# Two-layer hybrid decoder trunk: token norm in the operands of the mixer's second and later projections, convolution taps read from PSUM, o tiles before the convolved ones

## The chip, the cores and the metric

The kernel runs on one core of one Trainium2 chip. The metric is the device time of one execution in microseconds (us). The core's engines are TensorE (PE; its weight loads appear as PEld), VectorE (DVE), ScalarE (ACT), GpSimd (POOL) and SyncE (SP, which here only issues loads and stores).

## What is computed

Input `x` has 512 tokens of width 1024. Each of two layers does

```
x += 1/2 * SwiGLU(RMSNorm(x))
x += W_out [ sparse-attention heads | mLSTM heads ](RMSNorm(x) @ W_in)
x += 1/2 * SwiGLU(RMSNorm(x))
```

The mixer (the second line) is what the change touches. In the reference, cut to what matters:

```
q, k, v, q_idx, k_idx, w_idx, qk_m, v_m, o_m, i_pre, f_pre = split_columns(h @ w_in)      # h = rmsnorm(x, g)
att = dsa_attention(rope(rmsnorm(q)), rope(rmsnorm(k)), v, rope(q_idx), rope(k_idx), w_idx)  # top-128 keys per query
qk_m = silu(causal_conv(qk_m, conv_w, conv_b))                                            # 4 taps along the tokens
h_m = mlstm(q_m, k_m, v_m, i_pre + b_i, f_pre + b_f)                                      # 4 heads, chunks of 128
h_m = rmsnorm(h_m, m_norm) * sigmoid(o_m)
return concatenate([att, h_m]) @ w_out
```

with `rmsnorm(x, g) = x * rsqrt(mean(x*x) + eps) * g`. The factor `rsqrt(...)` is one number per token, the gain `g` one per channel.

## The kernel before

**Layout.** `x` is held transposed, eight tiles `x[i]` of 128 channels x 512 tokens. Every fp32 matmul is done as three matmuls (`mm3`, line 296) over operands split in a high and a low part (`hi`, `lo`; `whi`, `wlo` for weights, `yh`, `yl` for the normed input). Weights come in units of 128 x 1024. SP loads each unit into `raw`; ACT rounds it to `whi`; `wlo` is made by DVE, or (units marked for it, all of the mixer but the first four) by an ACT copy and a load that POOL issues and that adds the weights to it (`unit`, line 263).

**The mixer** (`mixer`, line 545) runs in this order:

1. `norm` (line 315): per tile ACT squares `x[i]` and writes `yh = x*g`, DVE writes `yl = x*g - yh`, POOL adds the squares up in `acc`. The gain is in these operands, the token factor isn't.
2. `proj_a` (index and key columns, gates), `proj_q`, `proj_v`: each a `proj_tok` (line 574), four weight units of 8 tile pairs. In these the tokens are the output partitions. The token factor `rs` (one per partition) is applied when ACT takes the result out of PSUM.
3. Twelve `proj_chan` (line 921), one weight unit and 24 matmuls each, in the order `HEADS` (line 36): four o tiles and, per head, one tile for q and one for k. Here the tokens are the free dimension, and DVE multiplies the result by `rsb`, the token factor spread over all partitions. For an o tile ACT then takes a tanh (`proj_o`, line 931). For q and k (`proj_qk`, line 941) the product lands in a padded SBUF tile `cv`, ACT applies the last tap and the bias, DVE adds three taps, and ACT and DVE make the silu.
4. `out_proj` (line 1064) of the attention half, then of the mLSTM half, each 16 groups of 6 matmuls per half; DVE adds into `x`.

**What sets the order.** PE's instructions keep the order in which the program issues them; the other engines' are ordered by a scheduler that goes by program order, priorities and estimated times. Beside the main line there are threads (generators): the tail of the norm, `front` (index and key tiles, scores), `gates`, `qprep`, `select` (top 128 by 8 at a time), `attention`, and one `mlstm` per head. The main line calls `tick()` after every 6 matmuls, and each thread then runs on to its next `yield n`, which lets it sleep for n ticks (`LAG`, line 34). So the threads' PE instructions stand between those of the projections, at places counted in ticks. `drain()` and `join()` run ticks without matmuls of the main line.

The threads that matter here:

- `scale` (line 342) starts 12 ticks after `norm` (`LAG["norm"]`): four matmuls (eight PE instructions) over `acc`, `rsqrt` on DVE (11 small steps), four diagonal tiles; 3 ticks later a matmul spreads them, and ACT writes `rsb`.
- `front`: `prep(b)` rotates and splits the index and key columns of one block of 128 tokens into `stk` tiles; `flip` transposes them on PE. `prep(0)` is issued at tick 17, its flips at tick 24.
- `attention`: logits on PE, mask and minimum on DVE, exponential on ACT, transposes on PE, a copy `pT` on ACT, and two ticks after the transposes the product with v into `op`. Block results go to `zah`, `zal`.
- `mlstm(l, h)` (line 967) is spawned when both convolved tiles of head h are issued and waits until the head before it has got through. Its PE steps are `mb` at once, the two products on the convolved tiles 4 ticks later (`cv`), the chunk states 2 later, the first pair of outputs `hn` 2 later, the second pair 1 later. Then DVE and ACT normalize `hn` to `hm`, and 10 ticks after the second pair PE transposes `hm` (line 1054); from that `zh`, `zl`, the operands of the second half of the output projection, are made. The transposes also wait until all o and convolved tiles are issued.

PSUM: four banks `mm` serve the projections and `mlstm`, three `aux`, one `op`.

Of the kernel before, what the change touches and what calls it, by code (L numbers as in the profile page):

```python
# [7 lines left out]
F32 = mybir.dt.float32  # L8
F32R = mybir.dt.float32r
I32 = mybir.dt.int32  # L10
AF = mybir.ActivationFunctionType
ALU = mybir.AluOpType
# [3 lines left out]
P = 128  # L16
S = 512
# [3 lines left out]
NKT = D // P  # L21
# [5 lines left out]
MH, MD = 4, 128  # L27
# [3 lines left out]
FILL = -3.3e38  # L31
MARK = -3.4e38
UN = 1024
LAG = {"norm": 12, "prep": 3, "prep2": 4, "f0": 1, "q0": 12, "qprep": 5, "att": 2, "ml": 2, "cv": 4, "hm": 9,
       "gates": 16, "ffn": 6, "ffn0": 10, "bc": 4, "g": 5, "fl": 1, "sc": 1, "attend": 3, "np": 1}
HEADS = (("o", 0), ("qk", 0), ("qk", 1), ("qk", 2), ("o", 1), ("qk", 3), ("o", 2), ("o", 3))
PLAIN = ((0, 0), (0, 1), (1, 0), (1, 1))
H = S // 2
WARM = 16
# [5 lines left out]
POOLC = (0, 0)  # L45
# [14 lines left out]
class Trunk:  # L60
# [484 lines left out]
    def mixer(self, l):  # L545
        self.norm(self.gm[l])
        self.flips = 0
        self.fronted = False
        self.chosen = {0}
        self.conv = {}  # L550
        self.hm = {}
        self.z = {}
        self.va = None
        self.zatt = None
        self.attended = 0
        self.proj_a(l)
        self.proj_q(l)
        self.proj_v()
        self.ml = 0
        self.join(lambda: self.fronted)  # L560
        self.so = {}
        for nm, h in HEADS:
            if nm == "o":
                self.proj_o(h)
            else:
                self.proj_qk(l, h, 0)
                self.proj_qk(l, h, 1)
                self.spawn(self.mlstm(l, h))
        self.join(lambda: self.attended == NB)
        self.out_proj([(self.zatt[0][:, i, :], self.zatt[1][:, i, :]) for i in range(4)])  # L570
        self.drain()
        self.out_proj([self.z[h] for h in range(MH)])

    def proj_tok(self, n):
        ps = [self.pm.tile([P, S], F32, name="mm", tag="mm") for _ in range(NB)]
# [201 lines left out]
    def proj_q(self, l):  # L777
        nc = self.nc
        ps = self.proj_tok(512)
        self.qT = self.ap_.tile([P, AH, S], F32R, name="qT", tag="qT")  # L780
        qa = []
        for b in range(NB):
            qa.append(self.ap_.tile([P, S], F32, name="qa", tag="s4a", bufs=4))
            nc.scalar.activation(qa[b], ps[b], AF.Copy, scale=self.rs[:, b:b + 1])
        self.spawn(self.qprep(qa))

    def qprep(self, qa):
# [124 lines left out]
    def proj_v(self):  # L912
        nc = self.nc
        ps = self.proj_tok(512)
        self.va = self.ap_.tile([P, NB, MH, MD + 1], F32, name="va", tag="big")
        nc.gpsimd.memset(self.va[:, :, :, MD:MD + 1], 1.0)
        for b in range(NB):
            nc.scalar.activation(self.va[:, b, :, 0:MD], ps[b].rearrange("p (h d) -> p h d", d=MD), AF.Copy,
                                 scale=self.rs[:, b:b + 1])

    def proj_chan(self):
        hi, lo = self.unit()
# [8 lines left out]
    def proj_o(self, h):  # L931
        nc = self.nc
        ps = self.proj_chan()
        if h % 2 == 0:
            self.so2 = self.ap_.tile([P, 2, S], F32, name="so", tag="so", bufs=2)
        so = self.so2[:, h % 2, :]
        nc.vector.tensor_tensor(out=so, in0=ps, in1=self.rsb, op=ALU.mult)
        nc.scalar.activation(so, so, AF.Tanh, scale=0.5)
        self.so[h] = so

    def proj_qk(self, l, h, i):
        nc = self.nc
        ps = self.proj_chan()
        raw = self.ap_.tile([P, S + 4], F32, name="cv", tag="cv", bufs=2)
        nc.gpsimd.memset(raw[:, 0:3], 0.0)
        with self.tc.high_priority(offset=1500):
            nc.vector.tensor_tensor(out=raw[:, 3:3 + S], in0=ps, in1=self.rsb, op=ALU.mult)
            w = self.cw[l][:, i * MH + h, :]
            if i == 0:
                self.qk = self.ap_.tile([P, 2, S], F32, name="qk", tag="s4b", bufs=2)  # L950
            o = self.qk[:, i, :]
            nc.scalar.activation(o, raw[:, 3:3 + S], AF.Identity, scale=w[:, 3:4], bias=w[:, 4:5])
            for k in range(3):
                if POOLC[i] == 0:
                    nc.vector.scalar_tensor_tensor(o, raw[:, k:k + S], w[:, k:k + 1], o, op0=ALU.mult, op1=ALU.add)  # L955
                else:
                    t = self.tmp()
                    if POOLC[i] == 1:
                        nc.scalar.activation(t, raw[:, k:k + S], AF.Copy, scale=w[:, k:k + 1])
                    else:  # L960
                        nc.gpsimd.tensor_scalar(t, raw[:, k:k + S], w[:, k:k + 1], None, op0=ALU.mult)
                    nc.gpsimd.tensor_tensor(out=o, in0=o, in1=t, op=ALU.add)
            nc.scalar.activation(raw[:, 0:S], o, AF.Tanh, scale=0.5)
            nc.vector.scalar_tensor_tensor(o, raw[:, 0:S], 1.0, o, op0=ALU.add, op1=ALU.mult)
        self.conv[h, i] = o

    def mlstm(self, l, h):
# [181 lines left out]
```

## Time and profile before

| | |
|---|---|
| median of 3 runs | 1914.17 us (1914.05 to 1914.24) |
| the profiled execution's own time | 1914.28 us |
| its span in the profile | 1912.6 us |
| PE busy | 1893.8 us, 99% of the span |
| DVE busy | 1377.9 us, 72% |
| ACT busy | 961.4 us, 50% |
| POOL busy | 531.6 us, 28% |
| first mixer on PE | from 362 to about 613 us |
| second mixer on PE | from 1310 to about 1560 us |

A profile row names the source line, the engine, the operation and `output<-inputs` by tile names; a timeline row begins with start and duration in us and ends, in brackets, with the idle time of the engine just before it and what released it. Matmuls overlap one another, so the duration of one (0.39 us) is longer than the step from one to the next. Rows of a timeline merge equal neighbours (`x8`). The granted PE clock is 1.00 of full speed in all stretches of the mixers.

### The profile page before, as it was taken

To read this page: it belongs to the slowest core of one execution; us is meant where nothing else is said; L and a number is where in the kernel's file an instruction comes from. 1 tells how busy PE (TensorE), PEld (TensorE's weight loads), DVE (VectorE), ACT (ScalarE), POOL (GpSimd) and SP (SyncE) were. 2 spreads that over 40 slices of the span, in tenths; PEclk is the share of its full clock that TensorE was granted. 3 is DMA by queue.
4 is the path that set the end of the run, shared out by engine and by line. 5 is a ranking of instruction groups with operands and counts; after the bars stand their busy time and mean duration, and the time that the engine had idled before them with its cause. 6 is when DMAs were issued, how large, how long until landed. Compare 5 with 4: busy or idle time off the path is not lost.

```text
span 1912.6 us, 29533 instructions
## 1 busy us (share of the span) xinstructions
PE 1893.8 (99%) x11712; PEld 1700.5 (89%) x11712; DVE 1377.9 (72%) x2227; ACT 961.4 (50%) x1505; POOL 531.6 (28%) x328
## 2 busy tenths in 40 slices
PE   9999999999999999999999999999999999999999
PEld 7899999887888899999989999998878888999997
DVE  7966667589956786666787666675898558766665
ACT  6434344477775544343464343436777755434342
POOL 1432323212113242333224333312211122332430
PEclk9999999999999999999999999999999999999999
DMA  8232323365446632322362332334644455332322
GB/s 245 78 121 89 122 78 129 113 154 120 107 93 144 143 111 79 120 98 102 118 151 80 115 102 98 111 106 132 155 111 98 107 144 116 116 118 79 130 67 89
DMA packets 63067, 219.28 MB, mean 115 GB/s; under 512 B 8272, under 2 KB 8784, under 8 KB 62928
## 3 DMA queue, kind: packets, MB, share of 16 engines
q1 hardware_dynamic: 51120, 176.34, 27.2%
q0 software_dynamic: 11232, 40.90, 12.8%
q8 instruction: 92, 1.51, 0.3%
q14 instruction: 47, 0.39, 0.1%
q10 hardware_dynamic: 576, 0.15, 0.0%
HBM read 215.27 MB, written 2.10 MB: 114 GB/s over the span
## 4 chain that ended last, share of the span: by engine, by line
PE 90%; DVE 5%; ACT 2%; issue 1%; POOL 1%; DMA 1%; SPq 0%; ACTq 0%; DVEq 0%; POOLq 0%
PE mm L486 36%; PE aux L294 28%; PE mm L294 24%; PE op L294 2%; DVE wlo L277 1%; ACT whi L272 1%; PE aux L888 1%; DMA x<-x_dram 1%; POOL ws L249 1%; DVE qk L955 0%; DVE qT L392 0%; DVE sc L839 0%; ACT wlo L274 0%; DVE tmp L617 0%; DVE zal L471 0%
## 5 line engine op out<-in xcount | busy, mean ns | idle before, releaser
L272 ACT ACTIVATE whi<-raw 128x1024 fp32r<-128x1024 f32 (+1 forms) x292 | 308.2, 1056 | 443.9 <-PE aux L294 197.7
L277 DVE TENSOR_TENSOR wlo<-raw,whi 128x1024 fp32r<-128x1024 f32 (+1 forms) x214 | 286.3, 1338 | 100.8 <-ACT whi L272 97.5
L249 POOL TENSOR_TENSOR ws<-raw 128x1024 f32<-128x1024 f32 x72 | 194.4, 2700 | 544.8 <-DVE wlo L277 457.1
L486 PE MATMUL mm<-yh,whi 128*128 128x256 f32 x1152 | 326.3, 283 | 0.0
L486 PE MATMUL mm<-yh,wlo 128*128 128x256 f32 x1152 | 326.0, 283 | 0.0
L486 PE MATMUL mm<-yl,whi 128*128 128x256 f32 x1152 | 326.0, 283 | 0.0
L277 DVE TENSOR_TENSOR wlo<-ws,whi 128x1024 fp32r<-128x1024 f32 x144 | 220.3, 1530 | 95.5 <-ACT whi L272 95.3
L272 ACT ACTIVATE whi<-ws 128x1024 fp32r<-128x1024 f32 x144 | 152.7, 1061 | 263.7 <-PE mm L486 136.6
L486 PEld LDWEIGHTS mm<-yh,whi 128*128 128x128 f32 x1152 | 221.0, 192 | 1.5
L486 PEld LDWEIGHTS mm<-yl,whi 128*128 128x128 f32 x1152 | 221.0, 192 | 1.2
L486 PEld LDWEIGHTS mm<-yh,wlo 128*128 128x128 f32 x1152 | 221.0, 192 | 0.0
L542 DVE SCALAR_TENSOR_TENSOR x<-aux,x 128x512 f32<-128x512 f32 x192 | 130.6, 687 | 125.2 <-PE aux L294 124.8
L486 PE MATMUL mm<-qT,whi 128*128 128x256 f32 x1152 | 209.6, 284 | 0.4
L486 PEld LDWEIGHTS mm<-qT,whi 128*128 128x128 f32 x1152 | 182.0, 192 | 3.1 <-issue 0.9
L486 PE MATMUL mm<-qT,wlo 128*128 128x256 f32 x576 | 163.2, 283 | 0.0
L294 PE MATMUL aux<-zah,whi 128*128 128x512 f32 x384 | 149.8, 390 | 0.0
L294 PE MATMUL aux<-zal,whi 128*128 128x512 f32 x384 | 149.8, 390 | 0.0
L294 PE MATMUL aux<-zah,wlo 128*128 128x512 f32 x384 | 149.4, 389 | 0.0
L249 POOL TENSOR_TENSOR ws<-ws,raw 128x1024 f32<-128x1024 f32 x36 | 89.1, 2475 | 115.8 <-issue 111.5
L486 PEld LDWEIGHTS mm<-qT,wlo 128*128 128x128 f32 x576 | 110.7, 192 | 0.0
L486 PE MATMUL mm<-s4a,whi 128*128 128x256 f32 x576 | 106.3, 284 | 0.0
L294 PE MATMUL mm<-yh,whi 128*128 128x512 f32 x256 | 104.6, 409 | 0.0
(290 smaller groups left out, 4247.1 us busy)
## 6 DMA issues: line engine op xcount, KB each, us to landing
raw<-wg_dram SPq DMA_DIRECT2D x88, 512.0 KB, 3.5
raw<-wu_dram SPq DMA_DIRECT2D x88, 512.0 KB, 3.7
raw<-wdb_dram SPq DMA_DIRECT2D x80, 512.0 KB, 3.6
raw<-w_qk_dram SPq DMA_DIRECT2D x16, 512.0 KB, 3.2
wlo<-w_qk_dram POOLq DMA_DIRECT2D x16, 512.0 KB, 5.5
raw<-w_out_dram SPq DMA_DIRECT2D x16, 512.0 KB, 3.2
wlo<-w_out_dram POOLq DMA_DIRECT2D x16, 512.0 KB, 6.0
raw<-wda_dram SPq DMA_DIRECT2D x8, 512.0 KB, 3.4
```

Of the source, the lines that this page charges most:

```text
L249: self.tc.keep_in_program_order(self.nc.gpsimd.tensor_tensor(out=out, in0=x, in1=y, op=op))
L272: nc.scalar.activation(hi[:, :n], raw, AF.Copy)
L277: nc.vector.tensor_tensor(out=lo[:, :n], in0=raw, in1=hi[:, :n].bitcast(F32), op=ALU.subtract)
L294: self.nc.tensor.matmul(ps, lhsT, rhs, start=start, stop=stop)
L486: nc.tensor.matmul(ps[:, f, :], a[:, c], r, start=first and f == 0 and k == 0 and n == 0, stop=k == 3 and n == 2, skip_group_check=True)
L542: nc.vector.scalar_tensor_tensor(self.x[d], ps, 0.5, self.x[d], op0=ALU.mult, op1=ALU.add)
L888: nc.tensor.transpose(pt[:, j * P:(j + 1) * P], it["lg"][:, j * P:(j + 1) * P], self.ident)
```

## The change

Three things, all in the mixers:

- `LAG["norm"]` goes from 12 to 7, and after `proj_a` a new `normalize` makes `y` again, in place: DVE computes `x * g * rsb` into a temporary, ACT rounds it to `hi`, DVE subtracts for `lo`. From `proj_q` on, the operands hold the whole norm; the evictions of q and v lose their scale, the o and conv tiles their multiply by `rsb`.
- The convolution has no padded SBUF copy any more: ACT applies last tap and bias straight from PSUM, and the three DVE taps read PSUM, each on the columns that it has.
- `HEADS`, which orders both the tiles and their weight units, becomes o0, o1, o2, four q/k pairs, o3.

```
-LAG = {"norm": 12, ...
+LAG = {"norm": 7, ...
-HEADS = (("o", 0), ("qk", 0), ("qk", 1), ("qk", 2), ("o", 1), ("qk", 3), ("o", 2), ("o", 3))
+HEADS = (("o", 0), ("o", 1), ("o", 2), ("qk", 0), ("qk", 1), ("qk", 2), ("qk", 3), ("o", 3))
...
         self.proj_a(l)
+        self.join(lambda: self.normed)
+        self.normalize(l)
         self.proj_q(l)
...
+    def normalize(self, l):
+        nc = self.nc
+        for i in range(NKT):
+            t = self.tmp()
+            nc.vector.scalar_tensor_tensor(t, self.x[i], self.gm[l][:, i:i + 1], self.rsb, op0=ALU.mult, op1=ALU.mult)
+            hi, lo = self.y[i]
+            nc.scalar.activation(hi, t, AF.Copy)
+            nc.vector.tensor_tensor(out=lo, in0=t, in1=hi.bitcast(F32), op=ALU.subtract)
...
-            nc.scalar.activation(qa[b], ps[b], AF.Copy, scale=self.rs[:, b:b + 1])
+            nc.scalar.activation(qa[b], ps[b], AF.Copy)
...
-            nc.scalar.activation(self.va[:, b, :, 0:MD], ps[b].rearrange("p (h d) -> p h d", d=MD), AF.Copy,
-                                 scale=self.rs[:, b:b + 1])
+            nc.scalar.activation(self.va[:, b, :, 0:MD], ps[b].rearrange("p (h d) -> p h d", d=MD), AF.Copy)
...
-        nc.vector.tensor_tensor(out=so, in0=ps, in1=self.rsb, op=ALU.mult)
-        nc.scalar.activation(so, so, AF.Tanh, scale=0.5)
+        nc.scalar.activation(so, ps, AF.Tanh, scale=0.5)
...
-        raw = self.ap_.tile([P, S + 4], F32, name="cv", tag="cv", bufs=2)
-        nc.gpsimd.memset(raw[:, 0:3], 0.0)
...
-            nc.vector.tensor_tensor(out=raw[:, 3:3 + S], in0=ps, in1=self.rsb, op=ALU.mult)
...
-            nc.scalar.activation(o, raw[:, 3:3 + S], AF.Identity, scale=w[:, 3:4], bias=w[:, 4:5])
-            for k in range(3):
-                if POOLC[i] == 0:
-                    nc.vector.scalar_tensor_tensor(o, raw[:, k:k + S], w[:, k:k + 1], o, op0=ALU.mult, op1=ALU.add)
...
+            nc.scalar.activation(o, ps, AF.Identity, scale=w[:, 3:4], bias=w[:, 4:5])
+            for k in (2, 1, 0):
+                j = 3 - k
+                nc.vector.scalar_tensor_tensor(o[:, j:], ps[:, :S - j], w[:, k:k + 1], o[:, j:], op0=ALU.mult,
+                                               op1=ALU.add)
+            t = self.ap_.tile([P, S + 4], F32, name="cv", tag="cv", bufs=2)
+            nc.scalar.activation(t[:, 0:S], o, AF.Tanh, scale=0.5)
+            nc.vector.scalar_tensor_tensor(o, t[:, 0:S], 1.0, o, op0=ALU.add, op1=ALU.mult)
```

## Rows read from the trace of the kernel before

**Rows 1.** Waits, PE: for what, us in total, times, longest us.

```profile
PE op L294 <- ACT pT L891: 4.5, 6, 1.2
PE mm L294 <- DVE zal L864: 1.4, 2, 0.8
```

**Rows 2.** Timeline, PE, first mixer: a wait; ends of heads 2 and 3.

```profile
442.62 0.40 PE L294 MATMUL mm<-yh,wlo 128*128 128x512 f32 x1
444.18 0.43 PE L294 MATMUL op<-v,pT 128*128 128x64 f32 x2 [1.16 <-ACT pT L891]
...
553.40 0.47 PE L294 MATMUL mm<-yh,whi 128*128 128x512 f32 x1
...
574.09 0.47 PE L294 MATMUL mm<-zah,whi 128*128 128x512 f32 x1
...
587.80 0.60 PE L1054 MATMUL aux<-zid,hm 128*128 128x128 f32 x4
...
590.99 0.39 PE L294 MATMUL mm<-yh,whi 128*128 128x512 f32 x1
```

**Rows 3.** Chain that ended last: start, us, what (runs of equal matmuls).

```profile
362.31 14.88 PE mm L294 x72
...
588.40 32.68 PE mm L294 x144
```

**Rows 4.** Windows: stretch, length, busy us of PE, PEld, DVE, ACT, POOL, PEclk, DMA.

```profile
383.40:437.00 53.60, 53.60 (x275) 45.00 (x273) 45.33 (x169) 40.78 (x74) 10.91 (x13) 1.00 0.70 156
437.00:470.00 33.00, 30.42 (x171) 24.63 (x171) 32.56 (x93) 22.89 (x59) 6.86 (x10) 1.00 0.49 108
```

**Rows 5.** Lines by form: busy us, mean ns of one | idle before, releaser.

```profile
L955 DVE SCALAR_TENSOR_TENSOR qk<-cv,cw,qk 128x512 f32<-128x512 f32 x48 | 41.3, 861 | 2.3 <-ACT qk L952 1.8
L542 DVE SCALAR_TENSOR_TENSOR x<-aux,x 128x512 f32<-128x512 f32 x192 | 130.6, 687 | 125.2 <-PE aux L294 124.8
L947 DVE TENSOR_TENSOR cv<-mm,rsb 128x512 f32<-128x512 f32 x16 | 10.9, 681 | 1.4 <-PE mm L294 1.4
L374 DVE SCALAR_TENSOR_TENSOR ys<-x,g,rsb 128x512 f32<-128x512 f32 x32 | 22.9, 745 | 0.0
...
L391 ACT ACTIVATE yh<-ys 128x512 fp32r<-128x512 f32 x16 | 9.8, 622 | 2.0 <-DVE ys L374 1.8
```

**Rows 6.** Timeline, start of the first mixer: PE, POOL and DVE.

```profile
377.03 0.95 PE L294 MATMUL aux<-ones,tmp 128*128 128x1 f32 x8
394.67 1.10 PE L294 MATMUL aux<-zid,stk 128*128 128x256 f32 x8
...
367.88 1.31 POOL L331 TENSOR_TENSOR tmp<-tmp 128x512 f32<-128x512 f32 x1 [2.02 <-ACT tmp L329]
...
378.01 0.16 DVE L348 TENSOR_SCALAR nms<-aux 128x4 f32<-128x4 f32 x1 [7.25 <-PE aux L294]
385.55 0.17 DVE L639 TENSOR_SCALAR widx<-pa 128x16 f32<-128x16 f32 x1 [4.21 <-ACT pa L629]
393.29 0.29 DVE L671 TENSOR_TENSOR stk<-tmp,stk 128x128 fp32r<-128x128 f32 x1 [0.36 <-ACT stk L670]
```

**Rows 7.** Timeline, ACT and DVE, first mixer: `hn` to `hm`, then `zl`.

```profile
559.96 1.28 ACT L1048 ACTIVATE hm<-hn,m_rr 128x128 f32<-128x128 f32 x4 [0.33 <-DVE m_rr L1044]
575.48 0.37 ACT L1028 ACTIVATE hn<-mm 128x258 f32<-128x258 f32 x1
577.09 0.40 ACT L1040 ACTIVATE tmp<-hn,m_rd 128x128 f32<-128x128 f32 x1 [1.24 <-DVE m_rd L1036]
581.83 1.28 ACT L1048 ACTIVATE hm<-hn,m_rr 128x128 f32<-128x128 f32 x4
...
576.28 0.16 DVE L1032 TENSOR_SCALAR m_neg<-hn 128x4 f32<-128x4 f32 x1
580.45 0.68 DVE L1076 TENSOR_TENSOR x<-mm,x 128x512 f32<-128x512 f32 x1
590.08 0.75 DVE L1061 SCALAR_TENSOR_TENSOR yl<-tmp,mn,yh 128x512 fp32r<-128x512 f32 x1 [0.79 <-ACT yh L1060]
```

More of the change, by code (lines that the diff above doesn't have):

```diff
@@ L33 @@
 UN = 1024
-LAG = {"norm": 12, "prep": 3, "prep2": 4, "f0": 1, "q0": 12, "qprep": 5, "att": 2, "ml": 2, "cv": 4, "hm": 9,
+LAG = {"norm": 7, "prep": 3, "prep2": 4, "f0": 1, "q0": 12, "qprep": 5, "att": 2, "ml": 2, "cv": 4, "hm": 9,
        "gates": 16, "ffn": 6, "ffn0": 10, "bc": 4, "g": 5, "fl": 1, "sc": 1, "attend": 3, "np": 1}
-HEADS = (("o", 0), ("qk", 0), ("qk", 1), ("qk", 2), ("o", 1), ("qk", 3), ("o", 2), ("o", 3))
+HEADS = (("o", 0), ("o", 1), ("o", 2), ("qk", 0), ("qk", 1), ("qk", 2), ("qk", 3), ("o", 3))
 PLAIN = ((0, 0), (0, 1), (1, 0), (1, 1))
@@ L943, in proj_qk @@
         ps = self.proj_chan()
-        raw = self.ap_.tile([P, S + 4], F32, name="cv", tag="cv", bufs=2)
-        nc.gpsimd.memset(raw[:, 0:3], 0.0)
+        w = self.cw[l][:, i * MH + h, :]
+        if i == 0:
+            self.qk = self.ap_.tile([P, 2, S], F32, name="qk", tag="s4b", bufs=2)
+        o = self.qk[:, i, :]
         with self.tc.high_priority(offset=1500):
-            nc.vector.tensor_tensor(out=raw[:, 3:3 + S], in0=ps, in1=self.rsb, op=ALU.mult)
[L948 to L951, printed above, removed]
-            nc.scalar.activation(o, raw[:, 3:3 + S], AF.Identity, scale=w[:, 3:4], bias=w[:, 4:5])
-            for k in range(3):
-                if POOLC[i] == 0:
-                    nc.vector.scalar_tensor_tensor(o, raw[:, k:k + S], w[:, k:k + 1], o, op0=ALU.mult, op1=ALU.add)
[L956 to L964, printed above, removed]
+            nc.scalar.activation(o, ps, AF.Identity, scale=w[:, 3:4], bias=w[:, 4:5])
[6 more added lines that the diff above has]
+            nc.vector.scalar_tensor_tensor(o, t[:, 0:S], 1.0, o, op0=ALU.add, op1=ALU.mult)
         self.conv[h, i] = o
```

## The prediction

> **What bounds the kernel now.** I read the waits of TensorE (PE) first, then the stretches of one mixer, then the timelines at the places that the change touches. All times are of layer 0's mixer; layer 1 repeats them 947 us later, so each saving or loss counts twice.
>
> PE works almost without a gap. It waits for the attention's transposed weights `pT` six times, 4.5 us in all, and for `zal`, the first attention output, twice, 1.4 us [rows 1]. So there are 5.9 us of such waits in the two mixers, 2.95 us in each. The rows understate a wait slightly: the `op` matmul that waited 1.16 us started 1.56 us after its predecessor, where a step of 0.23 us is usual [rows 2, 3]. Its other waits lie in the feed-forward blocks, which the change leaves alone. In the stretch 437 to 470 us VectorE (DVE) is busy 32.6 of 33.0 us, and PE only 30.4; from 383 to 437 DVE has 8.3 us to spare [rows 4]. So DVE time matters only where PE ends up waiting for it. PE instructions keep the program's order, so a PE instruction that waits stops all of PE.
>
> PE's order comes from ticks: 6 matmuls make a tick. 72 of them take 14.88 us in the first projection, 1.24 us a tick, and 144 of the 512-wide ones take 32.68 us, 0.227 each and 1.36 us a tick [rows 3]. Counted from the start of the mixer, `proj_a`, `proj_q` and `proj_v` are ticks 1 to 48, the twelve `proj_chan` tiles 49 to 96, and the attention half of the output projection 97 to 112.
>
> **Part 1, fewer and cheaper operations in the conv and o tiles.** Per mixer 12 multiplies by `rsb` leave DVE (8 for the convolution, 4 for o), 0.681 each: 8.2 us [rows 5]. The 24 taps read PSUM in place of SBUF. From SBUF they average 0.861; the nearest 512-wide operation with one PSUM operand takes 0.687 [rows 5], so I take 4.2 us less; at worst they stay as they are. None of this is on PE's path by itself: the results are wanted several ticks later, and what it can buy is the waits of [rows 1].
> [...]
> The bank of a convolved tile is now held for one activation and three taps, some 0.7 + 3 x 0.69 = 2.8 us and the handoffs, in place of 0.68. Four banks serve these tiles and `mlstm`. A new tile is opened every 4 ticks, over 5.4 us, so I cost this at nothing; the cover is the banks that are free, and if it fails, once a mixer at most, 1.5 us.
>
> **Part 2, the norm put into the operands.** Added per mixer: 8 scalings on DVE at 0.745 and 8 subtractions at 0.68 (as the multiply by `rsb`, the same operation and shape), 11.4 us, and 8 copies on ScalarE (ACT) at 0.62, 5.0 us [rows 5]. Scaling and copies work in place on `y`, so they follow the last reader in `proj_a`. The lag of 7 for 12 puts the sum of squares (8 PE instructions, 0.95 us [rows 6]), the 11 small DVE steps of `rsqrt` and its four diagonals 5 ticks earlier. PE then wants `acc` at 362.31 + 7 x 1.24 = 371.0; POOL ends it at 367.88 + 1.31 = 369.2 [rows 3, 6]. No stall, 1.8 us to spare. `rsb` is there at about 377, before ACT's evictions of the first projection.
> DVE idled 7.25 us before 378.01 and 4.21 us before 385.55 [rows 6]. From 377 to 385.5 the scalings fill a stretch of 8.4 us whose own work has moved ahead; about 3 us are left over, and these push `prep(0)`. It ends at 393.58, and PE wants its tiles at 394.67: 1.1 us of slack [rows 6]. Pushed by 3 us, PE would stall 1.9 us; pushed by nothing, 0. The second `prep` and the gates run in the same stretch and can give way, so I take 0.3, near the lower end. Of the wait for normalized `y0`, `y1` at the start of `proj_q` I expect nothing: they have 6 us from `rsb`. If ACT's evictions get in front, 1 us.
>
> **Part 3, the order of the tiles.** o, o, o, then the convolved pairs, then o. Weight loads, their ACT copies and the loads that POOL issues keep number and size at every position (an o unit is as large as a qk unit), so SP's and POOL's queues see only other addresses. The first head's `mlstm` is spawned after tick 68 in place of 60. A head takes 10 ticks from its first matmul to its last and waits for the one ahead; the four form a chain, and all of it comes 8 ticks later. The last head's second output pair is at tick 100 now and at 108 after; its transposes come 10 ticks later, 110 and 118. But the attention half ends at tick 112, and ticks 113 to 118 are the drain, without matmuls.
> Before: the last pair ends at 574.09 (the next matmul starts), `hm` is ready at 581.83 + 1.28 = 583.11, so that chain takes 9.0 us; its transposes are at 587.80 behind 10 ticks of matmuls, 4.7 us of slack [rows 2, 7]. After, only 4 ticks cover it: 24 x 0.227 = 5.4 us. **Stall: 9.0 - 5.4 = 3.5 us** (unrounded), for which PE has nothing else in its order. Lower bound: head 2's chain took from 553.40 to 561.24, 7.8 us [rows 2, 7], a stall of 2.4; the chain's own operations (the copy of 0.37, four small ones on DVE from 576.28 to 577.06, then 577.09 to 583.11 less the `x` add in between, some 0.6) come to 6.6, a stall of 1.2 [rows 7]. Upper: one more pair of weight copies, 2.1, gives 5.6. I take 3.5, the same head's row.
> Behind the transposes `zl` ends at 590.08 + 0.75 = 590.83, 3.0 after the transposes' start; 12 more matmuls of the attention half stood there before, now 9 of the second half only, 2.0 us and 0.4 of transposes. Its low part is the second of the three matmuls that use it, 0.2 later: **0.3 us** more (0 to 0.6).
> For the first head's start (matmul to exponentials to the state), 6 ticks and the rest cover the chain about as now: nothing, 0.5 us if ACT is late.
>
> **What comes back.** The ticks 49 to 64 hold three o tiles and one conv in place of one o and three, so DVE sheds most of its load where it is full, 437 to 470 [rows 4]. Two of the waits stand behind conv work there; the 1.16 at 444.18 [rows 2] stands before any of it. `zal`'s wait stood behind head 3's weights, which are 8 ticks later now. I take half of 2.95: **-1.5 us**; bounds 0 and all 2.95.
>
> **Sum.** Per mixer 3.5 + 0.3 + 0.3 - 1.5 = 2.6, for two 5.2. The profiled execution took 1914.28 us, 0.11 above the median: 1919.5 for it, 1919.4 for a median.
>
> **Rivals.**
> 1. *The relief wins: faster.* DVE, unloaded by part 1, lets every wait of [rows 1] go, and head 3's chain runs without gaps: a stall of 1.2 at the drain, -2.95, and 0.15 for each of eight understated waits: 2 x (1.2 - 2.95) - 1.2 = -4.7, 1909.6 us. It decides at the drain: the change gains once the stall there is less than what comes back. For it: DVE is full exactly where PE waits. Against: ACT makes its weight copies in the midst of that chain, and the first wait of [rows 2] precedes all that part 1 relieves. Chance 0.15.
> 2. *Both about cancel.* Stall 2.4 as head 2's chain, relief 2.4: 1914 us, between 1910.3 and 1918. Chance 0.30.
> 3. *The backlog bites too.* Scalings push `prep(0)` by the full 3 us (1.9), ACT delays `y1` (1.0), nothing of the waits returns: 2 x (3.5 + 0.3 + 1.9 + 1.0) = 13.4, 1927.7 us. For it: from 437 on DVE has nothing to spare, and the added 11.4 us come ahead of that. Against: 8.3 us are free in the stretch before. Chance 0.17.
> That the order is not as counted isn't likely: PE's order is written out, and the tick count meets the rows (10 ticks of 1.36 between pair and transposes).
>
> **How the numbers follow.** My own case has 0.38, with its range 1916 to 1923. A measurement here can tell about 0.2%, 3.8 us, from no change. Faster by more is rival 1, 0.15, slower by more is my case and rival 3 less a part that falls under 1918.0: 0.53; the rest, 0.32, is the same. The range holds rival 2, most of rival 3 and the edge of rival 1: 1910 to 1926.5; about 1 in 10 lies beyond either end.
>
> **What would show it.** Right: PE's wait of 2 to 5 us, twice, at the transposes of the last `hm` (line of the `mlstm` transposes, released by ACT `hm`), with the second output half straight behind; the multiplies by `rsb` gone; taps near 0.69; fewer waits `op` for `pT`; no wait for `acc`. Wrong: no PE wait there, which would mean the chain needs 5.4 us or less; or PE waits at the flips of the first `prep` or at `proj_q`'s first matmuls, which is rival 3; or new waits of conv or `mlstm` tiles for a bank.

## The result and the profile after

The changed kernel takes **1933.07 us** (1932.82 to 1934.10, 4 runs) beside 1914.11 us before (1913.12 to 1914.24, 4 runs): a ratio of 1.0104, 95% interval 1.0092 to 1.0115. It is slower by 19 us, 1.0%, and beyond the predicted range. Its profiled execution took 1932.82 us, its span is 1931.1 us. PE is busy for 1900.4 us, DVE 1383.6, ACT 970.3.

With `normalize` (lines 576 to 583) and the shorter convolution, a line of the mixer's later code has a number that is 1 to 11 higher than before. The waits of PE in the changed kernel (for what, us in total, times, longest), against [rows 1]:

```profile
PE mm L294 <- ACT yh L582: 10.1, 2, 5.1
PE aux L1055 <- ACT hm L1049: 4.9, 2, 2.5
...
PE op L294 <- ACT pT L902: 2.8, 4, 1.1
...
PE aux L294 <- DVE a_mn L916: 1.2, 2, 0.6
```

The attention's waits shrank, from 5.9 us to 4.0. Two new ones are larger than all that left: 5.1 us in each mixer for the first `yh` of the new operands, 2.5 us in each for the last `hm`. The timeline of the first mixer at these two places, PE, then ACT, then DVE, against [rows 2, 6]:

```profile
382.17 0.36 PE L294 MATMUL mm<-whi,yl 128*128 128x460 f32 x1
387.59 0.79 PE L294 MATMUL mm<-whi,yh 128*128 128x512 f32 x1 [5.06 <-ACT yh L582]
...
597.31 1.35 PE L1055 MATMUL aux<-zid,hm 128*128 128x128 f32 x4 [2.47 <-ACT hm L1049]
598.31 0.78 PE L294 MATMUL mm<-yh,whi 128*128 128x512 f32 x1
...
375.13 0.60 ACT L356 ACTIVATE rsb<-aux 128x512 f32<-128x512 f32 x1 [1.14 <-PE aux L294]
385.50 1.28 ACT L736 ACT_TABLE_LOAD   x1
386.80 0.22 ACT L736 ACTIVATE g_ex<-g_ab 128x16 f32<-128x16 f32 x1
386.92 1.13 ACT L582 ACTIVATE yh<-tmp 128x512 fp32r<-128x512 f32 x2
...
384.13 0.17 DVE L650 TENSOR_SCALAR widx<-pa 128x16 f32<-128x16 f32 x1 [10.37 <-ACT pa L640]
384.74 0.74 DVE L580 SCALAR_TENSOR_TENSOR tmp<-x,gm,rsb 128x512 f32<-128x512 f32 x1
```

`rsb` is there at 375.13 + 0.60 = 375.7, the scalings need nothing else, and DVE stands still for 10.37 us. The instruction at the head of its queue is `widx`, which wants the last eviction of the first projection. The first scaling stands five instructions behind it and starts at 384.74, nine microseconds after its operands were there. It ends at 385.48, but ACT makes the first copy only at 386.92: a table load of 1.28 us and an exponential of the gates stand in front.

The windows of that kernel (stretch, length, busy us of PE, PEld, DVE, ACT, POOL, granted PE clock, DMA share, GB/s) show a second loss, behind the wait:

```profile
382.60:387.60 5.00, 0.01 (x1) 0.01 (x1) 3.39 (x12) 4.97 (x10) 0.86 (x1) 0.77 0.90 201
387.60:391.60 4.00, 4.00 (x9) 2.98 (x10) 4.00 (x13) 3.95 (x6) 0.00 (x0) 0.50 0.66 135
...
598.00:600.00 2.00, 2.00 (x7) 1.60 (x7) 0.69 (x1) 0.71 (x2) 1.56 (x3) 0.50 0.90 182
```

The granted clock fell while PE stood still (0.77 in the mean of the first window, in which PE is busy for 0.01 us), and the matmuls behind ran at 0.50 of full speed: at 388.18 and 388.61 two of them start 0.43 us apart, at 392.11 and 392.34, with the clock back, 0.23. The same happens behind the wait for `hm` (0.50 from 598 to 600 us). In the second mixer the clock behind these two waits is 0.61 (1344.7 to 1348.7 us) and 0.66 (1555.4 to 1557.4). The lines by form (busy us, mean ns of one | idle before), against [rows 5]:

```profile
L961 DVE SCALAR_TENSOR_TENSOR qk<-mm,cw,qk 128x511 f32<-128x511 f32 x16 | 12.0, 748 | 14.5 <-ACT qk L958 14.5
L961 DVE SCALAR_TENSOR_TENSOR qk<-mm,cw,qk 128x509 f32<-128x509 f32 x16 | 11.9, 743 | 0.1
L961 DVE SCALAR_TENSOR_TENSOR qk<-mm,cw,qk 128x510 f32<-128x510 f32 x16 | 11.9, 743 | 0.1
L580 DVE SCALAR_TENSOR_TENSOR tmp<-x,gm,rsb 128x512 f32<-128x512 f32 x16 | 11.7, 744 | 0.0
L583 DVE TENSOR_TENSOR yl<-tmp,yh 128x512 fp32r<-128x512 f32 x16 | 10.7, 684 | 1.5 <-ACT yh L582 1.5
```

**How much, and where.** A mixer's length is here the time from the start of its first 460-wide matmul to that of the first matmul after its 768 in projections. Before, it is 612.75 - 362.15 = 250.60 us and 250.53 us; after, 621.11 - 360.78 = 260.33 and 260.98: 9.73 and 10.45 us more. These lengths leave out that the start of the first mixer varies by 1.5 us among all kernels of this study (360.70 to 362.23). But each is of one execution, the profiled one; where the executions of a kernel lie several us apart, its median over all of them says more.

### The profile page after: what moved, and what is told of

The parts are those of the page before. It is cut to its first block, busy times and chain, and to the rows that moved or that the text cites. A ratio compares the mean times of both kernels' runs of the same rounds, so it can differ in the third digit from the quotient of the medians.

```text
span 1931.1 us, 29551 instructions
## 1 busy us (share of the span) xinstructions
PE 1900.4 (98%) x11712; PEld 1704.9 (88%) x11712; DVE 1383.6 (72%) x2235; ACT 970.3 (50%) x1521; POOL 529.8 (27%) x312
## 4 chain that ended last, share of the span: by engine, by line
PE 86%; DVE 10%; ACT 2%; issue 1%; DMA 1%; POOL 1%; ACTq 0%; DVEq 0%; POOLq 0%
PE mm L486 35%; PE aux L294 26%; PE mm L294 21%; DVE sc L850 2%; DVE m L849 2%; PE op L294 1%; DVE wlo L277 1%; PE aux L899 1%; POOL ws L249 1%; ACT whi L272 1%; DVE sc L839 0%; DMA raw<-wu_dram 0%; ACT wlo L274 0%; DMA row<-nrow_dram 0%; DVE lg L916 0%
```

## The experiments

Theory A: the scalings' place in DVE's queue makes the first wait. Theory B: the order of the tiles makes the second. C: the waits themselves make the slow clock. The last two columns are the mixers' lengths in the profiled execution over those of before.

| kernel | us | ratio, interval | mixer 1 | mixer 2 |
|---|---|---|---|---|
| changed | 1933.07 | 1.0104 (1.0092 to 1.0115) | 9.73 | 10.45 |
| early | 1925.80 | 1.0062 (1.0049 to 1.0076) | 5.36 | 7.28 |
| oldheads | 1926.85 | 1.0067 (1.0053 to 1.0081) | 6.87 | 6.27 |
| early_oldheads | 1917.23 | 1.0019 (1.0010 to 1.0028) | 3.78 | 1.14 |
| bnewheads | 1917.68 | 1.0022 (1.0013 to 1.0031) | 1.48 | 1.54 |
| fill | 1930.88 | 1.0092 (1.0077 to 1.0108) | 9.01 | 8.99 |
| copyfirst | 1934.12 | 1.0106 (1.0092 to 1.0120) | 10.97 | 10.45 |
| split_oldheads | 1922.38 | 1.0048 (1.0035 to 1.0060) | 4.93 | 4.91 |
| split_midheads | 1923.16 | 1.0050 (1.0038 to 1.0063) | 4.44 | 5.66 |
| before_p8 | 1936.67 | 1.0121 (1.0108 to 1.0135) | 11.53 | 11.69 |
| split_oldheads_p8 | 1936.32 | 1.0120 (1.0106 to 1.0134) | 11.65 | 11.65 |
| split_oldheads_p6 | 1938.10 | 1.0127 (1.0113 to 1.0141) | 12.68 | 11.83 |
| split_midheads_p8 | 1951.38 | 1.0195 (1.0181 to 1.0209) | 18.54 | 18.63 |
| woven_oldheads | 1923.79 | 1.0051 (1.0037 to 1.0064) | 7.24 | 5.08 |
| woven_oldheads_n6 | 1921.82 | 1.0042 (1.0030 to 1.0055) | 2.97 | 4.07 |
| woven_midheads_n6 | 1921.14 | 1.0041 (1.0027 to 1.0054) | 4.12 | 4.87 |
| early_oldheads_n6 | 1914.52 | 1.0009 (0.9999 to 1.0018) | 0.87 | 0.86 |
| early_midheads_n6 | 1914.91 | 1.0007 (0.9998 to 1.0016) | 0.61 | 1.31 |
| early_oldheads_n5 | 1917.84 | 1.0022 (1.0014 to 1.0031) | 2.68 | 2.48 |

**1. The scalings earlier in the program (early).** In `proj_a`, ahead of the evictions; the two lines leave `mixer`.

```
         ps = self.proj_tok(C_A)
+        self.join(lambda: self.normed)
+        self.normalize(l)
```

> The changed kernel with the eight scalings put between the first projection's matmuls and its evictions in the program, so that VectorE's queue has them ahead of the index-weight operation that waits for the last eviction; the same operations, none added. Theory A (the scalings stand in VectorE's in-order queue behind an operation that waits for ScalarE's last eviction; that is the 5.06 us wait at the second projection's first matmul, and the slow matmuls after it are its consequence): the wait goes, the granted clock stays at 1.00 there, and the time falls by 2 x (5.06 + 2.2) = 14.5 us, to about 1918.6 us; the drain's wait of 2.5 us at the last transposes stays. Rival A' (the copies on ScalarE are too late in any order, because they share it with eight evictions and two weight copies): a wait of 2 to 3 us stays at the second projection, for yh or for a bank whose eviction now comes later, and the time falls to 1924 to 1928 us. Rival A'' (the lag of the norm or the scaling itself is what is late): no change, 1933 us.

1925.80 us, 7.3 us less than the changed kernel's median: rival A'. The first scaling now starts at 376.81 us, right behind `rsb`. PE no longer waits for `yh`, but the second bank of the second projection now waits for its eviction. PE's waits in this kernel:

```profile
PE mm L294 <- ACT v L641: 4.6, 2, 2.3
PE aux L1055 <- ACT hm L1049: 4.9, 2, 2.5
```

Theory A named the first obstacle rightly and missed that ACT's queue holds a second one.

**2. The old order in the changed kernel (oldheads), the new order in the kernel before (bnewheads), and both of the first edits (early_oldheads).**

```
-HEADS = (("o", 0), ("o", 1), ("o", 2), ("qk", 0), ("qk", 1), ("qk", 2), ("qk", 3), ("o", 3))
+HEADS = (("o", 0), ("qk", 0), ("qk", 1), ("qk", 2), ("o", 1), ("qk", 3), ("o", 2), ("o", 3))
```

> The changed kernel with the order of the tiles of before (one o tile, three convolved pairs, o, a pair, two o tiles); the rest as changed. Theory B (the new order moves the last head's chain against the drain: a wait of 2.5 us at its transposes, 0.3 us behind it, and 1.5 to 2 us in which the matmuls after the wait run at half the granted clock): the wait at the transposes goes and the time falls by 2 x (2.5 + 0.3 + 1.5) = 8.6 us, to about 1924.5 us; the wait at the second projection stays at 5.1 us. If the new order also gives the relief at the attention's waits, the waits for pT grow by up to 1.5 us a mixer and the time is 1925 to 1927.5 us. Rival (the wait at the drain comes from VectorE's later work of the added scalings, not from the order): the wait stays and the time is 1932 to 1934 us.

> The kernel before with nothing changed but the order of the tiles: o, o, o, the four convolved pairs, o. Theory B: the drain's wait appears here too, 2.5 to 3.5 us at the last transposes (in this kernel the last head's chain has the multiplies by the norm and so is no shorter), 0.3 us behind it and 1.5 us at half clock, 4.3 to 5.3 a mixer; the relief at the attention's waits gives 0 to 1.5 us back: 1914.1 + 2 x (2.8 to 5.3) = 1919.7 to 1924.7 us, the likeliest 1922 us. Rival (the order costs nothing by itself; the drain's wait comes from the operands' part): 1911 to 1915 us.

> Both edits: the scalings ahead of the evictions in the program, and the order of the tiles of before. If theories A and B are right and add up: 1933.1 - 14.5 - 8.6 = 1910 us, up to 1914 us if the relief at the attention's waits is lost with the order; no PE wait above 1.5 us is left in the mixers. If part of the first wait stays (rival A'), 1916 to 1920 us. If the two are not independent (the scalings, now earlier, push the preparation of the index tiles, which then waits at the flips), 1914 to 1918 us with a new wait at the flips.

PE's waits in oldheads, then in bnewheads, then a window of bnewheads behind the wait for `hm`:

```profile
PE mm L294 <- ACT yh L582: 10.1, 2, 5.1
...
PE op L294 <- ACT pT L902: 3.6, 6, 1.1
...
PE mm L294 <- DVE zal L875: 0.8, 1, 0.8
```

```profile
PE aux L1054 <- ACT hm L1048: 4.9, 2, 2.5
PE op L294 <- ACT pT L891: 2.9, 4, 1.2
```

```profile
589.30:591.50 2.20, 1.89 (x8) 1.30 (x9) 0.65 (x1) 1.14 (x4) 1.86 (x3) 1.00 0.88 250
```

Theory B holds as to the wait: it comes and goes with the order alone, and is the same 2.5 us in both kernels. What it costs is less clear. In its profiled execution the kernel with only the new order has no slow clock behind the wait and loses 1.5 us a mixer, under the 2.8 that was expected at least. That execution took 1915.87 us and was the second shortest of ten; they lie between 1915.69 and 1920.65, with a mean granted clock that falls from 0.999 to 0.995 as the time grows. By their median the order costs (1917.68 - 1913.48) / 2 = 2.1 us a mixer. Taking the order out of the changed kernel gives 9.73 - 6.87 = 2.9 and 10.45 - 6.27 = 4.2 us a mixer. With the order of before, parts 1 and 2 together cost 6.9 and 6.3 us.

early_oldheads ends at 1917.23 us, above the 1910 to 1914 of theories A and B, in the 1916 to 1920 of rival A', and 15.8 below the changed kernel; what is left is the wait for the bank. Why it is there, in that kernel's timeline, ACT, then PE:

```profile
384.03 1.05 ACT L272 ACTIVATE whi<-raw 128x1024 fp32r<-128x1024 f32 x1
384.98 0.62 ACT L580 ACTIVATE yh<-tmp 128x512 fp32r<-128x512 f32 x1
385.49 1.05 ACT L274 ACTIVATE wlo<-whi 128x1024 fp32r<-128x1024 f32 x1
386.44 0.62 ACT L580 ACTIVATE yh<-tmp 128x512 fp32r<-128x512 f32 x1
386.96 0.30 ACT L641 ACTIVATE v<-mm,nrs 128x64 f32<-128x64 f32 x1
...
387.32 0.50 PE L294 MATMUL mm<-whi,yh 128*128 128x512 f32 x1 [2.32 <-ACT v L641]
```

**3. Matmuls that nobody reads, put into the two waits (fill).**

```
+    def fill(self, n):
+        pt = self.pa.tile([P, S], F32, name="aux", tag="aux")
+        for _ in range(n):
+            self.mm(pt[:, 0:384], self.zid[:, 0:P], self.zid[:, 0:384], True, True)
...
         self.normalize(l)
+        self.fill(29)
         self.proj_q(l)
...
+        if h == MH - 1:
+            self.fill(13)
         pt = self.pa.tile([P, S], F32, name="aux", tag="aux")
```

> The changed kernel with matmuls added that nobody reads: 29 of 384 columns ahead of the second projection and 13 ahead of the last head's transposes, in both mixers. By the steps of 0.227 us for 512 columns and 0.207 for 460 they take some 0.17 us each, 4.9 and 2.2 us, less than the waits of 5.4 and 2.6 us in which they stand. Theory C (the half-clock matmuls behind each wait come from TensorE having stood still): the granted clock stays at 1.00 there, and the time falls although 84 matmuls are added: 2 x (2.2 + 1.5) = 7.4 us less, 1925.7 us. If only the first place counts, 1928.7 us. Rival (the slow stretch comes with the place: fresh operands, the transfers of that stretch): the matmuls behind the waits stay at half clock, 1933 us. If the added ones delay what stands behind them, above 1933 us.

The windows at the same two places:

```profile
387.90:391.60 3.70, 3.46 (x15) 2.45 (x15) 3.70 (x12) 3.65 (x7) 0.00 (x0) 1.00 0.71 146
...
597.50:602.00 4.50, 4.42 (x18) 3.04 (x19) 1.57 (x3) 1.62 (x5) 2.32 (x4) 1.00 0.91 196
```

Theory C holds as to the cause: with PE kept at work the clock stays at 1.00, the operands and transfers being the same. The time fell by 2.2 us only, where 7.4 were expected. By ticks, in the first mixer 1.6 us were won at the second projection, and 1.4 of them went again at the flips of the second index tile, which now came before their operands were ready:

```profile
404.51 0.72 PE L294 MATMUL aux<-zid,stk 128*128 128x256 f32 x4 [1.12 <-DVE stk L719]
```

So in the changed kernel the slow matmuls cover work that is late anyway. That led to the next question: how late are the index tiles?

**4. Copies y2 to y7 behind the evictions (split_oldheads; split_midheads with two o tiles in front and two behind).** On the early kernel, with the order of before or the order between:

```
-        self.normalize(l)
+        self.normalize(l, range(0, 2))
         a = self.ap_.tile([P, NB, C_V], F32, name="pa", tag="big")
...
+        self.normalize(l, range(2, NKT))
         ss = self.small([P, NB], "kss")
```

> The run with both edits, and the eight scalings and copies parted: y0 and y1 ahead of the first projection's evictions in the program, y2 to y7 behind them; the same operations. The run with both edits still waited 2.32 us at the seventh matmul of the second projection, for the eviction of the second bank (ScalarE had put the copies of y4 to y7 and two weight copies in front of it), and ten matmuls after that wait ran at half clock. Theory: with the evictions in front of y2 to y7 that wait goes with its slow matmuls, 2 x (2.5 + 1.5) = 8 us less than 1917.2 us: about 1909.5 us, faster than the kernel before by some 4 us. Rival 1: y2, y3 come too late instead, for the seven or more operations that ScalarE now has in front of them; a wait of 1 to 2 us at the 25th matmul of the second projection, 1912 to 1915 us. Rival 2: the squares and so the first index tiles are later, a wait of 1 to 2 us at the flips, 1912 to 1915 us.

> As the run with the parted scalings, with an order between the two: two o tiles, the four convolved pairs, two o tiles. The last head's chain is then covered by 4 ticks more than in the changed kernel (24 matmuls of 0.227 us, 5.4 us, against a wait of 2.5 us). Theory: no wait at the last transposes, and the relief at the attention's waits that came with two o tiles in front stays in part: 0 to 1.5 us a mixer less than with the old order, so about 1908 us. Rival: the waits for pT are as with the old order and the tighter chain of heads adds some, 1910 to 1913 us.

1922.38 us is 5 us more than with everything ahead of the evictions. Rival 2 was right in kind and too small: the bank's wait is gone, and PE waits at the first flips instead, 3.04 us in the first mixer and 4.55 in the second. DVE ends the last `yl` only at 387.45 + 2.50 = 389.95; before, it took up `widx` and then the preparation at 385.55 [rows 6]. The order between gave nothing beyond the old one.

**5. The flips later, by 4 ticks (p8) or 2 (p6).**

```
-... "prep": 3, "prep2": 4, ...
+... "prep": 3, "prep2": 8, ...
```

> The run with the parted scalings and the old order, with the flips of the index tiles 4 ticks later (24 matmuls, 5.4 us, of the second projection are put ahead of them). Without that the run waited at those flips, 3.04 and 4.6 us in the two mixers, and the matmuls behind ran at half clock; by ticks it lost 5.5 and 6.5 us there against the kernel before. Theory D (the eleven microseconds of scalings and subtractions delay the first index tiles by some 5.5 us whatever stands ahead, and that is the second half of the loss): with 5.4 us of matmuls in front the wait is 0 to 1 us, and the time falls by 8 to 12 us, to 1911 to 1915 us, less if the later scores push the attention's waits. Rival (the flips are late for the gates' table loads, which move along with them): a wait of 2 us or more stays at the flips, 1916 us or more.

> The same with the flips 2 ticks later (2.7 us of matmuls in front). Theory D: of 3.3 us some 0.6 stay in the first mixer and 2 in the second, with some of the slow matmuls: 1922.4 - 2 x 3 = 1916 us, between the run without and the run with 4 ticks. If the attention's waits grow with each tick, this one is the better of the two.

> The parted scalings, the order between (two o tiles, four pairs, two o tiles), and the flips 4 ticks later. Theory D: as with the old order, 1911 to 1915 us, the waits for pT and zal smaller by what the two o tiles in front give (the run without the ticks had 2.7 and 1.2 us of such waits in place of 3.6 and 0.8), so within 1 us of it.

> The kernel before with nothing changed but the flips of the index tiles 4 ticks later: a control. There was no wait at the flips, so there is nothing to gain; if what follows them (scores, selection, attention) has room, 1913 to 1915 us; if the attention's half of the output projection is reached too early for it, up to 4 x 1.36 = 5.4 us more a mixer, 1925 us. What it costs here is to be taken off the gain of the others.

All of these missed, the control too: it lost 23 us. The wait at the first flips did go in split_oldheads_p8, but a wait of up to 7.1 us for a bank that holds scores came up in the third projection, and such waits make the same 16.8 us in all in both kernels. split_midheads_p8 has 17.1 us of them and waits 5 us a mixer for `zah`; split_oldheads_p6 still waits 1.4 and 1.5 us at the first flips and 12.6 us for the scores. PE's wait in the control, then ACT and DVE in its timeline:

```profile
PE aux L294 <- ACT tmp L823: 16.8, 4, 7.1
```

```profile
424.82 0.49 ACT L823 ACTIVATE tmp<-aux 128x384 f32<-128x384 f32 x1 [8.62 <-DVE sc L826]
...
421.50 0.41 DVE L839 MATCH_REPLACE8 sc<-m,sc 128x256 f32<-128x256 f32 x1
423.85 0.87 DVE L826 TENSOR_SCALAR sc<-tmp,widx 128x384 f32<-128x384 f32 x1
```

ACT waits for DVE's `sc`, which stands in DVE's queue behind the selection steps of the block before and the work on q. Later flips are no way out, and these runs can't say what the operand part costs where the flips have time.

**6. y4 to y7 only behind the preparation of the first index tile (woven), and the norm a tick or two earlier (n6, n5).** For woven on the split kernel, where y2 and y3 stay behind the evictions; for the others on early_oldheads, and on the same with the order between:

```
         prep(0)
+        self.normalize(l, range(4, NKT))
         yield LAG["prep"]
...
-LAG = {"norm": 7, ...
+LAG = {"norm": 6, ...
```

> The old order of the tiles; y0 and y1 scaled ahead of the first projection's evictions, y2 and y3 behind them, y4 to y7 only behind the preparation of the first index tile; the same operations as in the changed kernel. Place theory (the loss is where the added operations stand in the in-order queues: first ahead of y0, then ahead of the banks, then ahead of the first index tile; each place can be left): VectorE's work ahead of the first flips falls by 8 of 16 operations, 5.7 us, and the wait of 3 to 4.6 us there goes; what is left is 0 to 2 us a mixer: 1912 to 1917 us, the likeliest 1915 us. Load theory (ScalarE is full from the norm to the flips, with 5 us of copies added to evictions, three pairs of weight copies and the gates' table loads, so that something is late in any order): a wait of 2 to 4 us a mixer comes back at y4 or at the flips, 1918 to 1923 us.

> The same with the norm begun one tick earlier (lag 6 for 7): all of this is 1.24 us earlier, and acc is ready 0.5 us before TensorE wants it. Place theory: up to 1.2 us a mixer less than the run without, if something still waits there; the same if nothing does. Load theory: 1.2 us and its share of slow matmuls, some 2 us a mixer, less than the run without.

> The woven scalings and the earlier norm with the order between (two o tiles, four pairs, two o tiles). No wait at the last transposes; within 1 us of the same kernel with the old order; it shows what the order is worth when the first projections are not what is late.

> All scalings ahead of the evictions with the old order (1917.2 us) and the norm begun one tick earlier. Its wait of 2.32 us at the second bank should fall by 1.24 us or less, with some of the ten slow matmuls behind it: 1.2 to 2.5 us a mixer, 1912 to 1915 us. If the wait hangs on the end of the first projection and not on the norm, 1917 us.

> All scalings ahead of the evictions, the old order, the norm begun one tick earlier still (lag 5). In the run with lag 6 the waits for the banks were 0.29 and 0.49 us a mixer, 0.46 and 0.66 with what surrounds them. If they hang on the norm, they go: 2 x 1.1 less than 1914.5 us, 1912.3 us. Against it acc, ended by GpSimd, is then late by some 0.7 us, and TensorE waits for it once a mixer: 1913.7 us, and 1915 us or more if the matmuls behind that wait run slowly. A tie with the kernel before within 0.2% either way.

> All scalings ahead of the evictions, the norm at lag 6, the order between (two o tiles, four pairs, two o tiles). No wait at the last transposes, since 24 matmuls more stand ahead of them; the waits at the attention as in the other runs with this order (2.7 for pT, 1.2 for a_mn and 0.6 for yl in both mixers, against 3.6 for pT and 0.8 for zal with the old order): 1914.5 us within 1 us. If the order between were worth what the changed kernel's part 3 was meant for, 1911 to 1913 us.

The woven kernels go with the load theory: the wait moves once more, to the flips of the second block (3.05 us) in the first mixer, and stays at the first block (3.6 us) in the second. One window of the kernel before and two of woven_oldheads show what is full:

```profile
377.00:395.00 18.00, 18.00 (x86) 15.13 (x86) 10.44 (x58) 16.11 (x35) 2.60 (x3) 1.00 0.79 176
```

```profile
377.00:395.00 18.00, 18.00 (x87) 15.50 (x86) 13.31 (x42) 17.14 (x36) 2.59 (x3) 1.00 0.83 185
395.00:401.00 6.00, 3.08 (x16) 2.27 (x14) 4.78 (x16) 5.69 (x11) 0.86 (x1) 0.93 0.63 157
```

ACT rather than DVE: it had 1.9 us of 18 to spare before and gets 5 us of copies on top, beside three table loads of 1.28 us for the gates (387.42, 393.00 and 395.14 us), which it had before too. That is read from busy times; no run here takes work off ACT. What helps is to begin earlier. early_oldheads_n6 starts the norm one tick sooner, and no wait of PE in the mixers is longer than 1.1 us; the longest in sum:

```profile
PE op L294 <- ACT pT L902: 3.6, 6, 1.1
PE mm L294 <- ACT v L641: 1.6, 4, 0.5
```

It takes 1914.52 us beside 1912.98, an interval that holds no change: 18.6 us better than the changed kernel, and not better than the one before. The order between ties with it. A second tick (lag 5) is too much: `acc` is late by 0.7 us, as was feared, and the bank's wait is 1.60 us again, which was not; why it came back stays open. So no version tried here beats the kernel before.

**7. PSUM copied to SBUF ahead of the taps (copyfirst).**

```
+            t = self.ap_.tile([P, S + 4], F32, name="cv", tag="cv", bufs=2)
+            nc.scalar.activation(t[:, 0:S], ps, AF.Copy)
-            nc.scalar.activation(o, ps, AF.Identity, scale=w[:, 3:4], bias=w[:, 4:5])
+            nc.scalar.activation(o, t[:, 0:S], AF.Identity, scale=w[:, 3:4], bias=w[:, 4:5])
...
-                nc.vector.scalar_tensor_tensor(o[:, j:], ps[:, :S - j], w[:, k:k + 1], o[:, j:], op0=ALU.mult,
+                nc.vector.scalar_tensor_tensor(o[:, j:], t[:, :S - j], w[:, k:k + 1], o[:, j:], op0=ALU.mult,
...
-            t = self.ap_.tile([P, S + 4], F32, name="cv", tag="cv", bufs=2)
```

> The changed kernel with each convolved tile copied from PSUM to SBUF by ScalarE first (16 copies of about 0.6 us in all, 8 a mixer), and the last tap on ScalarE and the three on VectorE reading that copy, in the same shapes. By the rows of the two kernels (taps from SBUF 0.748 us where nothing disturbs them and 0.861 in the mean, from PSUM 0.745) VectorE gains nothing, and ScalarE's chain is 0.6 us longer a tile: 1932 to 1936 us, the likeliest 1934 us. [...]

1934.12 us beside 1933.07: for the time the copy makes no difference that can be told. The taps got no shorter; lines by form of this kernel:

```profile
L963 DVE SCALAR_TENSOR_TENSOR qk<-cv,cw,qk 128x511 f32<-128x511 f32 x16 | 14.9, 934 | 8.1 <-ACT qk L960 8.0
L963 DVE SCALAR_TENSOR_TENSOR qk<-cv,cw,qk 128x509 f32<-128x509 f32 x16 | 12.7, 793 | 0.2
L963 DVE SCALAR_TENSOR_TENSOR qk<-cv,cw,qk 128x510 f32<-128x510 f32 x16 | 11.9, 746 | 0.3
```

From SBUF the three taps average 0.82 us, from PSUM 0.745. 42 of the 48 take 0.73 to 0.75 us, as from PSUM; the other six take 1.1 to 1.75, each beside an operation of POOL (the last section). With three taps behind it the copy gained nothing.

## Why the prediction was wrong, step by step

The direction was right, the size was not: 2.6 us a mixer were predicted, 9.7 and 10.5 came. Counted by matmuls of the projections, the changed kernel is 7.5 us behind the kernel before at the end of the second projection, in both mixers: 5.2 by the wait for `yh`, for which nothing was taken, and 2.2 by what comes behind it, mostly slow matmuls. The order of the tiles makes the rest, 2.3 and 3.0 us.

- **Failed: part 2, "Of the wait for normalized `y0`, `y1` at the start of `proj_q` I expect nothing: they have 6 us from `rsb`."** `rsb` was there in time (375.7 us, 377 was taken), and the durations were right (0.744, 0.684, 0.62). But DVE's idle stretches of [rows 6] were taken for free time. They are waits of the instruction at the head of DVE's queue, and the scalings stood behind it there: in the changed kernel DVE stood still for 10.37 us before `widx`, and the first scaling started at 384.74, nine microseconds after `rsb`. The row showed the name that mattered, `widx<-pa`. The wait was 5.06 us in place of 0. In early, where the same scalings are issued ahead of that instruction, it is gone. The prediction did name the obstacle, "If ACT's evictions get in front, 1 us", at a fifth of its size.
- **Not priced: the clock.** Behind the wait the matmuls ran at a granted clock of 0.50 (387.6 to 391.6 us); in fill, where PE was kept at work, it stayed at 1.00 there. At the second projection the slow stretch hid lateness of the flips, so that it was worth 0.2 us net there, and 0.6 and 1.3 us at the drain.
- **Part 2, `prep(0)`**: priced at 0.3, at most 1.9. In the changed kernel it costs nothing, since PE arrives late itself. Where PE isn't late, it costs 3 to 4.6 us (split_oldheads). The sum was made against DVE's spare time; by busy time ACT was the fuller engine.
- **Part 3**: the wait at the drain has 2.47 us, near the lower bound of 2.4 and below the 3.5 taken (9.02 less 5.45 is 3.57). Head 3's chain is about as long as head 2's, 5.4 + 2.47 = 7.9 us against 7.8. Behind it, `zl` was no wait of its own. The order alone costs 1.5 us a mixer in the profiled execution and 2.1 by the median, against 3.5 + 0.3 - 1.5 = 2.3: right in kind and near in size.
- **What comes back**: the attention's waits lost (5.9 - 4.0) / 2 = 1.0 us a mixer, 1.5 were taken; with the order alone (bnewheads, 2.9 left) they lost the 1.5. One wait of the mixers was overlooked, and it went too, 0.37 us a mixer in the kernel before:

```profile
PE aux L294 <- ACT qT L712: 0.7, 2, 0.4
```

- **Part 1**: the twelve multiplies are gone; taps take 0.745, not 0.687, so 48 x (0.861 - 0.745) = 5.6 us of DVE are saved where 8.4 were taken. The mean of 0.861 was no price of reading SBUF (the last section). No wait for a bank by the longer hold, and none for `acc`: right.
- **Rivals**: the third, "the backlog bites too", named the place (ACT in front of `y1`, the flips) and gave 1.0 and 1.9 us, and 0.17 of chance. It came nearest, with its terms too small (1.0 where 5.06 stood) and without the clock. Part of its nearness is luck: the 1.9 us at the flips, which it counts, did not come in the changed kernel.

## What to carry to other kernels

Before work is put into an idle stretch of an engine, read what the engine is waiting for: here the 10.37 us in which DVE stood idle belonged to `widx`, the instruction at the head of its queue, and the scalings behind it got none of that time. When one obstacle is removed, ask which engine is full in that stretch; here ACT was (busy for 17.14 of 18 us in woven_oldheads), and the wait moved from `yh` to a bank to the index tiles. A wait of TensorE can cost more than its length (here 5.06 us, and the granted clock was 0.50 for 4 us behind it), so a sum over waits should ask of each whether the clock stays.

## What the runs showed of the hardware that was not expected

**The clock fell after some waits and not after others of the same length.** The wait of 2.5 us for `hm` was followed by a lower clock in both mixers of the changed kernel (0.50 from 598 to 600 us) and by 1.00 in both of the profiled execution of bnewheads (589.3 to 591.5). The bank's wait in early, 2.32 us in both mixers, was followed by full speed in the first and by 0.57 in the second:

```profile
387.20:391.00 3.80, 3.79 (x17) 3.15 (x18) 3.03 (x15) 3.77 (x14) 0.39 (x1) 1.00 0.88 163
...
1341.00:1343.00 2.00, 2.00 (x7) 1.57 (x6) 1.84 (x12) 1.98 (x11) 0.00 (x0) 0.57 1.05 152
```

In early_oldheads it was the other way round (0.50 from 388 to 390 us, 1.00 from 1339 to 1341). Nor is it fixed by the kernel: the ten executions of bnewheads, one program, have mean granted clocks from 0.999 down to 0.995 and differ by 5 us; where the clock fell in the other nine isn't known. The slow matmuls explain, at least in part, why the order cost 2.9 and 4.2 us in the profiles of the changed kernel and 1.5 in the other: without them it gained 0.6 and 1.3 at the drain (fill). What decides whether the clock falls stays open. After the waits of 1.2 us [rows 2, 4] and, in the first mixer, of 1.60 us (early_oldheads_n5, 386.4 to 388 us) it stayed at 1.00.

**Taps with two SBUF operands took up to 2.39 us beside an operation of POOL.** Of the 48 taps behind the mean of 0.861 [rows 5], 42 take 0.73 to 0.75 us and six take 1.05 to 2.39. In the kernel before, DVE and POOL, then in the changed kernel:

```profile
461.68 0.74 DVE L955 SCALAR_TENSOR_TENSOR qk<-cv,cw,qk 128x512 f32<-128x512 f32 x1
462.68 2.38 DVE L955 SCALAR_TENSOR_TENSOR qk<-cv,cw,qk 128x512 f32<-128x512 f32 x1
...
462.75 1.06 POOL L614 TENSOR_TENSOR tmp<-qa,qtab 128x256 f32<-128x256 f32 x1
463.45 1.06 POOL L615 TENSOR_TENSOR tmp<-qa,qtab 128x256 f32<-128x256 f32 x1
```

```profile
561.66 0.74 DVE L961 SCALAR_TENSOR_TENSOR qk<-mm,cw,qk 128x509 f32<-128x509 f32 x1
...
561.41 1.34 POOL L997 TENSOR_TENSOR qk<-qk,wi 128x384 f32<-128x384 f32 x1
```

The tap of 2.38 us ends half a microsecond after POOL's two operations do. So does each of the six long ones: all overlap an operation of POOL and end 0.54 to 0.56 us after it, while none of the 42 others overlaps more than the issue of a load. In the changed kernel, with one input in PSUM, none is longer than 0.75 us: the four such taps that run beside `qk<-qk,wi` take 0.74 us, and the means are 743 to 748 ns in all three shapes. Why the six end behind POOL's operation these runs don't show.
